# Hybrid encoder trunk: the gated branch's four tiles go straight into the projections' operand buffers

## The chip, the core and the metric

The kernel runs on one core of a Trainium2 chip. The core has five engines, each with an instruction queue that is worked off in order: PE (matrix multiplies, with its weight loads shown as PEld), DVE (elementwise and reductions), ACT (activation functions and copies with a scale), POOL (a slower elementwise engine) and SP, whose queue here only issues DMA transfers. The metric is the device time of one execution in microseconds (us); less is better.

## The reference, cut to what matters

One layer over 2048 frames of 1024 channels. Three branches (attention, a gated spatial MLP, an RWKV-7 recurrence) come out of one input projection; each is multiplied by a SiLU gate, projected to the model width, weighted by a sigmoid and summed.

```python
u, v = split(gelu(p))                       # branch B: 4 groups of 128 channels
s = einsum('gts,bnsgc->bntgc', w, layernorm(v)) + b_s
y_gm = u * s
branches = stack([y_mla, y_gm, y_rw], axis=2) * silu(z)
proj = einsum('bsnw,nwd->bsnd', branches, w_br)      # three projections, 512 -> 1024
merged = sum(proj * sigmoid(g_logit), axis=2)
x = x + gate * rmsnorm(merged @ w_out, post_g)
```

## The kernel before

**Tiling.** The 2048 frames go in four blocks `s` of 512; a tile is 128 channels by 512 frames of float32 (256 KB). Precision is kept by splitting each operand into a high and a low part: a product is three matmuls (`mm3`: high by high, high by low, low by high). `br_split` makes the parts of a projection's operand, `brh` by a copy with a scale on ACT and `brl` by a subtraction on DVE, in the pool `brp` with four buffers of each.

**Stages.** For each block there is a recurrence stage `wkv(s)` and then an attention stage `attention(s)`. Both are chains with waits in them, so a queue of independent work, `later`, is run beside them: a unit of `later` is a generator that yields wherever PE may change to another thread. The units of one queue run one after the other. In `wkv(s)` the queue holds the rest of block `s-1` (`finish_units`: `merge`, `out0`, `out1`, which end in the thread `rows`), then block `s`'s gated branch: for each group `g` the units `ug` (load the spatial result `sg_d`, compute u, multiply) and `zg` (compute the gate, multiply, store), then `operand` and eight `part` units, each a gate (24 matmuls on the 512-frame hidden state `hh`/`hl`) and a projection (12 matmuls on `brh`/`brl`).

**Order.** A planner, `Pace`, simulates the engines while the program is written out and decides which thread goes next. PE, whose order is fixed by hand, and SP's queue then run in the order that it chose. All loads and stores named here are on SP's queue; weight tiles `wh` and `wl` are prefetched there through three buffers, so an issue of a weight load waits until PE has used an older one, and everything behind it in the queue waits too.

**The lines around the change.** The unit that brings a stored branch back, used for the gated branch with `yg_d`, is

```python
def operand(src, b):
    yield ()
    for g in range(4):
        y = sm.tile([P, 512], F32, tag="z2", name="yg", bufs=3)
        SY.dma_start(y, src[g])
        b.append(br_split(y))
```

The tile `ut` that holds a gated tile has one buffer. `rows` is the end of block `s-1`: eight times it loads a tile `y` and a tile `x`, combines them on DVE, and stores `out`, with three buffers for the loads; `wkv(s)` lasts until it is done, and the attention's first loads (`stg`) are queued on SP behind its last store.

Of the kernel before, what the change touches and what calls it, by code (L numbers as in the profile page):

```python
# [11 lines left out]
F32 = mybir.dt.float32  # L12
# [9 lines left out]
P = 128  # L22
D = 1024
T = 2048
SB = 512
NSB = T // SB
# [280 lines left out]
def trunk(ctx, tc, io, out):  # L307
    nc = tc.nc
    pace = Pace()
    V, A, G, PE, SY = (pace.engine(e) for e in (nc.vector, nc.scalar, nc.gpsimd, nc.tensor, nc.sync))  # L310
    ctx.enter_context(tc.manual_schedule(engines={mybir.EngineType.PE}))

    def pool(name, bufs=1, space=None, stack=ctx):
        kw = {} if space is None else {"space": space}
        return pace.pool(stack.enter_context(tc.tile_pool(name=name, bufs=bufs, reuse_waits="tile", **kw)), bufs)
# [13 lines left out]
    dr = pool("dr", 1, DRAM)  # L329
# [250 lines left out]
    def gemm(w, c0, rhs, nk=KD, r0=0):  # L580

        yield (RD, *rhs[0])
        pace.lock = pace.cur
        o = pd()
        for kg in range(nk // 4):
            pace.early = EAR
            src = w[r0 + kg * 512:r0 + (kg + 1) * 512, c0:c0 + P].rearrange("(k p) c -> p k c", p=P)
            h, l = wgran((w.tensor.name, w.offset, r0 + kg * 512, c0), lambda raw: SY.dma_start(raw, src))
            pace.early = 0.0
            pace.forget(h, l)  # L590
            for k in range(4):
                kk = kg * 4 + k
                rh, rl = rhs[kk]
                yield (rh, rl)
                mm3(o, h[:, k, :], l[:, k, :], rh, rl, kk == 0, kk == nk - 1)
        pace.lock = None
        return o

    def silu2(n, f):

        o = yield from gemm(w_in, O_Z + n * 512 + f * P, hT)
        t = sm.tile([P, 512], F32, tag="gt", name="zt", bufs=2)
        A.activation(t, o, AF.Tanh, scale=0.5)
        z = sm.tile([P, 512], F32, tag="z2", name="z2", bufs=3)
        V.scalar_tensor_tensor(z, t, 1.0, o, op0=ALU.add, op1=ALU.mult)
        return z

    def br_split(b2, pl=brp):

        h = pl.tile([P, 512], F32R, tag="brh", name="brh", bufs=4)  # L610
        l = pl.tile([P, 512], F32R, tag="brl", name="brl", bufs=4)
        A.activation(h, b2, AF.Copy, scale=0.5)
        V.scalar_tensor_tensor(l, b2, 0.5, h.bitcast(F32), op0=ALU.mult, op1=ALU.subtract)
        return h, l
# [88 lines left out]
    yo_d = [dr.tile([8, P, SB], F32, name=f"yo_d{i}") for i in range(NSB)]  # L703
    y_d = [dr.tile([SB, D], F32, name=f"y_d{i}") for i in range(NSB)]
    yr_d = [dr.tile([4, P, SB], F32, name=f"yr_d{i}") for i in range(NSB)]
    yg_d = [dr.tile([4, P, SB], F32, name=f"yg_d{i}") for i in range(NSB)]

    def trig_of(s, pl):

# [200 lines left out]

        return [lambda f=f: vproj(f) for f in range(4)] + [vnorm] + [lambda g=g: spatial(g) for g in range(4)]

    def gm_gates(s):

        t = {}

        def ug(g):
            t[g] = sm.tile([P, 512], F32, tag="ut", name="ut", bufs=1)
            SY.dma_start(t[g], sg_d[s][g])
            o = yield from gemm(w_in, O_U + g * P, hT)  # L920
            u = sm.tile([P, 512], F32, tag="gt", name="gu", bufs=2)
            A.activation(u, o, AF.Gelu)
            V.tensor_tensor(out=t[g], in0=t[g], in1=u, op=ALU.mult)

        def zg(g):
            z = yield from silu2(1, g)
            V.tensor_tensor(out=t[g], in0=t[g], in1=z, op=ALU.mult)
            SY.dma_start(yg_d[s][g], t[g])

        return [f for g in range(4) for f in (lambda g=g: ug(g), lambda g=g: zg(g))]  # L930


    def latents():
# [15 lines left out]
    def wkv(s):  # L949
# [6 lines left out]
        with ExitStack() as st:  # L956
            pl = pool("wkv", 1, stack=st)
# [346 lines left out]

            rest = deque(later)
            later.clear()
            groups = (finish_units(s - 1, pl) if s else []) + [gm_gates(s) + branch(yg_d[s], s, 1)]
            for u in groups:
                later.append(u[0])
                for _ in range(GAP):  # L1310
# [219 lines left out]
    def gate(n, d):  # L1530
        og = yield from gemm(w_in, O_G + n * D + d * P, hT)
        t = sm.tile([P, 512], F32, tag="gt", name="gt", bufs=2)
        A.activation(t, og, AF.Tanh, scale=0.5)
        return t
# [5 lines left out]
    def part(n, s, d, br):  # L1540

        if n == 2:
            yield (lambda: s == NSB - 1 or old.get("turn", 0) > s,)
            t = sm.tile([P, 512], F32, tag="gt", name="gt", bufs=2)
            SY.dma_start(t, gd[s % 2][1][d])
            q = sm.tile([P, 512], F32, tag="z2", name="p1", bufs=3)
            SY.dma_start(q, pp[s % 2][0][d])
        else:
            t = yield from gate(n, d)
        op = yield from gemm(w_br[n], d * P, br, nk=4)  # L1550
        V.scalar_tensor_tensor(t, t, 1.0, op, op0=ALU.add, op1=ALU.mult)
        if n == 2:
            G.tensor_tensor(out=t, in0=t, in1=q, op=ALU.add)
        SY.dma_start(pp[s % 2][n - 1][d], t)
# [7 lines left out]
# [7 lines that stand above are left out]
# [5 lines left out]
    def branch(src, s, n):  # L1574

        b = []
        return [lambda: operand(src, b)] + [lambda d=d: part(n, s, d, b) for d in range(8)]
# [140 lines left out]
    with ExitStack() as st:  # L1718
        pl = pool("first", 1, stack=st)
# [5 lines left out]
    for s in range(NSB):  # L1725
        wkv(s)
        later.extend([lambda: mark(s)] + branch(yr_d[s], s, 2) + [lambda: mark(s, 2)])
        if s + 1 < NSB:
            attention(s, None)
        else:  # L1730
            with ExitStack() as st:
                bp = pool("brl", 1, stack=st)
                b0 = attention(s, bp)
                finish(s, b0)
# [23 lines left out]
```

## Time and profile before

| what | value |
|---|---|
| median of three runs | 3120.82 us (3120.63 to 3137.46) |
| the profiled execution | 3130.59 us, its span 3128.7 us |
| engines busy | PE 93%, DVE 55%, ACT 39%, POOL 19% of the span |
| DMA moved | 654.24 MB, mean 209 GB/s |
| mean granted clock of PE | 0.966 of full speed |

The span is from the first to the last instruction of the profiled execution; it is 1.9 us shorter than that execution's device time, which is itself 9.8 us (0.3%) above the median. A busy share is an average over stages; what a wait costs is read in its stage. In a timeline, a number in brackets at the end of a row is the time for which that engine sat idle before the instruction, with what ended it.

### The profile page before, as it was taken

What the parts mean: (1) busy time and instruction counts of PE and PEld (TensorE: products, weight loads), DVE (VectorE), ACT (ScalarE), POOL (GpSimd) and SP (SyncE); (2) the same over time, 40 slices, a digit from 0 to 9 for tenths busy, and PEclk for the clock granted to TensorE, in tenths of its full rate; (3) what the DMA queues carried; (4) which work ended last, traced back from release to release, by engine and by line L of the source; (5) the groups of instructions that cost most, each with busy time, mean ns of one, the idle gap of its engine ahead of it and who ended that gap; (6) DMA issues with size and microseconds to landing.
All of it is one profiled execution on the core that took longest, in us unless ns stands there. A gap on an engine that the chain in (4) does not pass through costs nothing.

```text
span 3128.7 us, 49533 instructions
## 1 busy us (share of the span) xinstructions
PE 2896.8 (93%) x16924; PEld 2337.8 (75%) x16924; DVE 1711.0 (55%) x4574; ACT 1231.6 (39%) x2866; POOL 595.7 (19%) x606
## 2 busy tenths in 40 slices
PE   5889898989989989999999998998999999899998
PEld 4667666778867767888867776887787677688886
DVE  6426666356356733467357653446645666266552
ACT  4325333444233423454233322554433333266641
POOL 3123232341121201122011101113100110122210
PEclk8999999989999989999999999999999999999999
DMA  8887765877676678766665577655557547844356
GB/s 272 264 274 240 225 191 167 281 251 242 222 221 196 196 229 280 219 205 191 212 199 174 165 243 251 207 167 188 154 170 243 182 149 227 272 151 129 125 181 208
DMA packets 525993, 654.24 MB, mean 209 GB/s; under 512 B 142673, under 2 KB 255405, under 8 KB 525741
## 3 DMA queue, kind: packets, MB, share of 16 engines
q1 hardware_dynamic: 525568, 651.03, 65.8%
q8 instruction: 134, 2.20, 0.3%
q14 instruction: 119, 0.97, 0.1%
q10 hardware_dynamic: 172, 0.05, 0.0%
HBM read 461.88 MB, written 189.01 MB: 208 GB/s over the span
## 4 chain that ended last, share of the span: by engine, by line
PE 40%; DVE 4%; DMA 3%; ACT 1%; issue 1%; SPq 1%; POOL 1%; POOLq 0%; DVEq 0%; ACTq 0%
PE pd L120 23%; PE pss L120 7%; PE pst L120 6%; PE pso L120 3%; SPq L120 1%; DVE X L120 1%; DVE tx L120 1%; DMA x<-in_x 1%; DMA yg<-yg_d 0%; DMA stg<-kp_d 0%; DMA tg<-gate_d 0%; DVE brl L120 0%; DMA stg<-q_d 0%; DMA yg<-mg_d 0%; POOL rs L120 0%
## 5 line engine op out<-in xcount | busy, mean ns | idle before, releaser
L120 PE MATMUL pd<-hh,wh 128*128 128x512 f32 x1952 | 811.3, 416 | 20.1 <-ACT wh L120 7.1
L120 PE MATMUL pd<-hh,wl 128*128 128x512 f32 x1952 | 774.9, 397 | 9.3 <-POOL wl L120 5.7
L120 PE MATMUL pd<-hl,wh 128*128 128x512 f32 x1952 | 771.7, 395 | 2.4 <-DVE hl L120 1.5
L120 PEld LDWEIGHTS pd<-hh,wh 128*128 128x128 f32 x1952 | 373.1, 191 | 112.1 <-issue 18.7
L120 PEld LDWEIGHTS pd<-hh,wl 128*128 128x128 f32 x1952 | 371.4, 190 | 98.8 <-POOL wl L120 9.8
L120 PEld LDWEIGHTS pd<-hl,wh 128*128 128x128 f32 x1952 | 373.2, 191 | 70.6 <-DVE hl L120 3.3
L120 DVE TENSOR_TENSOR pw<-pst,ph 128x512 fp32r<-128x512 f32 (+2 forms) x352 | 196.3, 568 | 246.0 <-ACT ph L120 244.7
L120 PE MATMUL pd<-brh,wh 128*128 128x512 f32 x576 | 259.5, 450 | 51.0 <-ACT brh L120 20.4
L120 ACT ACTIVATE ph<-pst 128x512 fp32r<-128x512 f32 (+2 forms) x352 | 171.5, 497 | 230.6 <-PE pst L120 199.1
L120 PE MATMUL pd<-brl,wh 128*128 128x512 f32 x576 | 236.3, 410 | 0.4 <-DVE brl L120 0.4
L120 PE MATMUL pd<-brh,wl 128*128 128x512 f32 x576 | 235.0, 408 | 0.5 <-DMA wl<-kept 0.5
L120 ACT ACTIVATE p<-p,nm 128x512 f32<-128x512 f32 (+3 forms) x288 | 189.9, 661 | 90.5 <-DVE nm L120 90.2
L120 DVE TENSOR_SCALAR_CACHE_REDUCE p<-pss 128x512 f32<-128x512 f32 (+2 forms) x320 | 191.1, 606 | 50.0 <-PE pss L120 46.3
L120 POOL TENSOR_TENSOR wl<-wr,wh 128x512 fp32r<-128x512 f32 x98 | 129.5, 1323 | 447.3 <-ACT wh L120 357.8
L120 ACT ACTIVATE wh<-wr 128x512 fp32r<-128x512 f32 x162 | 101.3, 628 | 215.7 <-PE pd L120 75.1
L120 PEld LDWEIGHTS pd<-brh,wh 128*128 128x128 f32 x576 | 113.5, 197 | 89.1 <-issue 25.0
L120 PE MATMUL pst<-consts,p 128*128 128x128 f32 x1088 | 162.5, 274 | 6.8 <-DVE t L120 3.7
L120 PE MATMUL pso<-ph,v 128*128 128x256 f32 x576 | 153.2, 288 | 0.5 <-ACT ph L120 0.5
L120 PE MATMUL pso<-pw,v 128*128 128x256 f32 x576 | 146.5, 283 | 0.1
L120 PEld LDWEIGHTS pst<-consts,p 128*128 128x128 f32 x1088 | 128.7, 141 | 23.6 <-issue 5.4
L120 POOL TENSOR_TENSOR kl<-stg,kh 96x512 fp32r<-96x512 f32 x80 | 103.3, 1293 | 210.1 <-ACT kh L120 194.5
L120 PEld LDWEIGHTS pd<-brh,wl 128*128 128x128 f32 x576 | 113.7, 197 | 27.5 <-DMA wl<-kept 0.9
(293 smaller groups left out, 4833.7 us busy)
## 6 DMA issues: line engine op xcount, KB each, us to landing
wh<-kept SPq DMA_DIRECT2D x486, 256.0 KB
wl<-kept SPq DMA_DIRECT2D x486, 256.0 KB
kept<-wh SPq DMA_DIRECT2D x162, 256.0 KB
kept<-wl SPq DMA_DIRECT2D x162, 256.0 KB
wr<-in_w_in SPq DMA_DIRECT2D x120, 256.0 KB
gate_d<-gt SPq DMA_DIRECT2D x64, 256.0 KB
part_d<-gt SPq DMA_DIRECT2D x64, 256.0 KB
p<-part_d SPq DMA_DIRECT2D x64, 256.0 KB
```

What stands on the lines that cost most here:

```text
L120: r = f(*a, **k)
```

## The change

`zg` no longer stores its tile to `yg_d`. It splits the tile into `brh` and `brl` at once and appends the pair to the list that the `part` units read. The unit `operand` is gone for this branch, and with it the reload; the other branches keep theirs. The tensor `yg_d` goes.

```diff
-    yg_d = [dr.tile([4, P, SB], F32, name=f"yg_d{i}") for i in range(NSB)]
-    def gm_gates(s):
-        t = {}
+    def gm_branch(s):
+        t, b = {}, []
         def zg(g):
             z = yield from silu2(1, g)
             V.tensor_tensor(out=t[g], in0=t[g], in1=z, op=ALU.mult)
-            SY.dma_start(yg_d[s][g], t[g])
-        return [f for g in range(4) for f in (lambda g=g: ug(g), lambda g=g: zg(g))]
+            b.append(br_split(t[g]))
+        return [f for g in range(4) for f in (lambda g=g: ug(g), lambda g=g: zg(g))] + [lambda d=d: part(1, s, d, b) for d in range(8)]
-            groups = (finish_units(s - 1, pl) if s else []) + [gm_gates(s) + branch(yg_d[s], s, 1)]
+            groups = (finish_units(s - 1, pl) if s else []) + [gm_branch(s)]
```

The planner sees other instructions, so it writes another order. SP's queue at the end of the last recurrence stage before, from the store of the fourth gated tile to the attention's first load (`yr_d` is the recurrence branch, whose reload follows):

```order
L120 DMA yg_d_370<-ut 128x512
L120 DMA yg<-yg_d_370 128x512
L120 DMA wh<-kept 128x512
L120 DMA out<-y 128x512
L120 DMA wl<-kept 128x512
L120 DMA yg<-yg_d_370 128x512 x3
...
L120 DMA out<-y 128x512
L120 DMA wl<-kept 128x512
L120 DMA wh<-kept 128x512
L120 DMA yg<-yr_d_366 128x512
L120 DMA stg<-q_d_326 96x512
```

The same place now, from the load of the fourth `ut`:

```order
L120 DMA ut<-sg_d_342 128x512
L120 DMA wl<-kept 128x512
L120 DMA out<-y 128x512
L120 DMA y<-y_d_361 128x512
L120 DMA x<-in_x 128x512
...
L120 DMA out<-y 128x512
L120 DMA wh<-kept 128x512
L120 DMA yg<-yr_d_366 128x512
L120 DMA wl<-kept 128x512
L120 DMA stg<-q_d_326 96x512
```

The stores and reloads are gone from between the `out` stores, and the attention's first load is still behind the last `out`.

DVE's queue at the same place before, around the fourth gated tile:

```order
L120 TENSOR_TENSOR ut<-ut,gu 128x512
L120 TENSOR_TENSOR ut<-ut,z_27889 128x512
L120 SCALAR_TENSOR_TENSOR y<-y,ors,x 128x512
L120 SCALAR_TENSOR_TENSOR brl<-yg,brh 128x512 x4
L120 SCALAR_TENSOR_TENSOR gt<-gt,pd 128x512
L120 SCALAR_TENSOR_TENSOR y<-y,ors,x 128x512
```

And now:

```order
L120 TENSOR_TENSOR ut<-ut,gu 128x512
L120 SCALAR_TENSOR_TENSOR y<-y,ors,x 128x512
L120 SCALAR_TENSOR_TENSOR z_27864<-zt,pd 128x512
L120 TENSOR_TENSOR ut<-ut,z_27864 128x512
L120 SCALAR_TENSOR_TENSOR brl<-ut,brh 128x512
L120 SCALAR_TENSOR_TENSOR y<-y,ors,x 128x512
L120 SCALAR_TENSOR_TENSOR gt<-gt,pd 128x512
```

The four splits that stood together behind the reload are now one behind each tile's last product, each ahead of one of the `rows` combinations (`y<-y,ors,x`).

PE's queue before, around the first score matmuls (`kh,qh`) of the last attention stage:

```order
L120 MATMUL pd<-brl,wh 128x512
L120 MATMUL pd<-brh,wl 128x512
L120 MATMUL pd<-hh,wh 128x512
L120 MATMUL pd<-hl,wh 128x512
L120 MATMUL pd<-hh,wl 128x512
L120 MATMUL pss<-kh,qh 128x512
L120 MATMUL pss<-kl,qh 128x512
```

And now:

```order
L120 MATMUL pd<-hl,wh 128x512
L120 MATMUL pd<-hh,wl 128x512
L120 MATMUL pss<-kh,qh 128x512
L120 MATMUL pss<-kl,qh 128x512
L120 MATMUL pss<-kh,ql 128x512
L120 MATMUL pd<-hh,wh 128x512
L120 MATMUL pd<-hl,wh 128x512
L120 MATMUL pd<-hh,wl 128x512
L120 MATMUL pd<-brh,wh 128x512
```

Between the stage's last `Y` transposes and its first scores stood 165 + 12 + 24 + 12 + 3 matmuls of gemms (216); now there are 165 + 12 + 21 (198). In the third block it was 219 and is 198. In the second block two `part` units and a gate stood between the gated branch and the first scores, and now it is three and a gate. In the first block the last state chunk of the first head pair is followed, before its `Y` transposes, by 24 + 12 + 24 matmuls where there were 6; in return one later pair of heads has 12 state matmuls in a row with nothing between them, where it had 8.

## Rows read from the trace of the kernel before

**Rows 1.** The page, part 1: busy time, share of the span, instructions

```profile
PE 2896.8 (93%) x16924; PEld 2337.8 (75%) x16924; DVE 1711.0 (55%) x4574; ACT 1231.6 (39%) x2866; POOL 595.7 (19%) x606
```

**Rows 2.** DMA issues by line: count, size of each

```profile
yg_d<-ut SPq DMA_DIRECT2D x16, 256.0 KB
yg<-yg_d SPq DMA_DIRECT2D x16, 256.0 KB
```

**Rows 3.** The operand's `brl` splits: ns min/median/max, first and last start

```profile
L120 DVE SCALAR_TENSOR_TENSOR brl<-yg,brh x68: 669/692/1607, 383.9 to 2871.6; 128x512 fp32r<-128x512 f32 x68
```

**Rows 4.** What PE waited for, whole span: us in total, times, longest

```profile
PE pd L120 <- ACT brh L120: 20.4, 6, 10.7
```

**Rows 5.** PE's timeline, third block, end of the recurrence stage: start us, us

```profile
1894.82 0.39 PE L120 MATMUL pd<-hh,wl 128*128 128x512 f32 x1
...
1900.94 0.39 PE L120 MATMUL pd<-hh,wl 128*128 128x512 f32 x1
1912.00 0.79 PE L120 MATMUL pd<-brh,wh 128*128 128x512 f32 x1 [10.68 <-ACT brh L120]
...
1917.36 0.40 PE L120 MATMUL pd<-hh,wh 128*128 128x512 f32 x1
...
1927.02 0.50 PE L120 MATMUL pss<-kh,qh 96*128 96x512 f32 x1 [0.62 <-ACT kh L120]
```

**Rows 6.** SP's timeline, same stage: first and last `out`, reloads, first attention load

```profile
1854.50 0.34 SPq L120 DMA_DIRECT2D out<-y  x1
...
1905.84 1.40 SPq L120 DMA_DIRECT2D yg<-yg_d  x3
...
1912.70 0.32 SPq L120 DMA_DIRECT2D yg<-yg_d  x1
...
1918.56 0.34 SPq L120 DMA_DIRECT2D out<-y  x1
...
1920.94 0.42 SPq L120 DMA_DIRECT2D stg<-q_d  x1
```

**Rows 7.** PE's timeline, fourth block, end of the recurrence stage

```profile
2704.28 0.79 PE L120 MATMUL pd<-brh,wh 128*128 128x512 f32 x1 [5.24 <-ACT brh L120]
...
2707.41 0.79 PE L120 MATMUL pd<-brh,wh 128*128 128x512 f32 x1 [1.18 <-ACT brh L120]
...
2711.59 0.39 PE L120 MATMUL pd<-hh,wh 128*128 128x512 f32 x1
...
2723.55 0.49 PE L120 MATMUL pss<-kh,qh 96*128 96x512 f32 x1 [2.93 <-ACT kh L120]
```

**Rows 8.** SP's timeline, fourth block: first and last `out`, first attention load

```profile
2651.90 0.38 SPq L120 DMA_DIRECT2D out<-y  x1
...
2713.65 0.38 SPq L120 DMA_DIRECT2D out<-y  x1
...
2715.77 0.41 SPq L120 DMA_DIRECT2D stg<-q_d  x1
```

**Rows 9.** DVE's timeline, fourth block: the first two `rows` combinations

```profile
2649.87 0.74 DVE L120 SCALAR_TENSOR_TENSOR y<-y,ors,x 128x512 f32<-128x512 f32 x1
...
2657.43 0.74 DVE L120 SCALAR_TENSOR_TENSOR y<-y,ors,x 128x512 f32<-128x512 f32 x1
```

**Rows 10.** PE's timeline, second block: the first projection of the gated branch

```profile
1202.36 0.49 PE L120 MATMUL pd<-brh,wh 128*128 128x512 f32 x1 [0.41 <-ACT brh L120]
...
1207.06 0.79 PE L120 MATMUL pd<-brh,wh 128*128 128x512 f32 x1 [2.53 <-ACT brh L120]
...
1211.15 0.63 PE L120 MATMUL pd<-hh,wh 128*128 128x512 f32 x1
```

**Rows 11.** DVE's timeline, first block: a split of the gated branch

```profile
388.66 1.38 DVE L120 SCALAR_TENSOR_TENSOR brl<-yg,brh 128x512 fp32r<-128x512 f32 x1 [0.29 <-ACT brh L120]
```

**Rows 12.** PE's timeline, first block: the wait for `Y` of the first head pair

```profile
393.95 1.09 PE L120 MATMUL pss<-consts,Y 128*128 128x128 f32 x4 [8.17 <-DVE Y L120]
```

**Rows 13.** Ten us after the stop in the third block: PE, PEld, DVE, ACT, POOL, PEclk, DMA

```profile
1910.00:1920.00 10.00, 7.84 (x24) 5.62 (x25) 4.07 (x6) 2.53 (x4) 0.00 (x0) 0.69 0.75 269
```

## The prediction

> **What bounds the kernel now.** The page's first part comes first: PE is busy 93% of the span and DVE, next, 55% [rows 1]. Independent work is put beside both chains, so the change can pay only in those stretches where PE stood still or ran at a lower clock, and the question for each edit is whether PE waited for it. The second view is the list of PE's waits: the largest single group is PE waiting for `brh`, 20.4 us in 6 waits, the longest 10.7 [rows 4]. The third is PE's timeline, which tells whose `brh` that was. It is the gated branch's, and three blocks share it: 10.68 us in the third [rows 5], 5.24 and 1.18 in the fourth [rows 7], 0.41 and 2.53 in the second [rows 10]; that is 20.0 of the 20.4. In the first block no such wait shows; there PE stands 8.17 us for `Y` of the recurrence [rows 12]. The last view is SP's queue in the same stretches, since a reload is issued there among weight loads and the transfers of `rows`.
>
> The sum is made against the profiled execution, 3130.6 us; it lies 0.3% above the median of 3120.8, and I take the difference found on the one off the other. A change of under 1% (31 us) can hardly be told from none here.
>
> **What goes.** 16 stores and 16 reloads of 256 KB [rows 2], 8.4 MB of 654 MB. The 20 us above are their round trip: the fourth tile cannot be reloaded before its store has landed, and PE has only the first gate's 24 matmuls to do meanwhile. Bytes by themselves I price at nothing, since none of the waits above is for bandwidth as such; the range takes in what shorter queues would give.
>
> **What stays.** The 16 splits on ACT and DVE are the same operations on the same shapes, 0.69 us on DVE [rows 3]. They move from behind the reload to behind each tile's last product. In DVE's queue each now stands ahead of one of the `rows` combinations, so a late `brh` on ACT holds up `rows`. The price is between nothing and a split with a wait like the one of 0.29 us [rows 11], about 1.0 us each, at most eight times in the last two blocks: 0 to 8 us. I take 0, because the four splits stood in the same queue before, in a clump, and waited there too. SP's wait for the last product and for the landing of the store goes with the store; `ut` is now released by the split, not by the store's landing. Four buffers of each half are filled one after the other while the gates are computed; the queue of independent work is one thread, so no other branch asks for them meanwhile, and nothing is priced for that.
>
> **Second block.** The first projection's 12 matmuls begin at 1202.36 after 0.41 us of waiting and the next gate begins at 1211.15 [rows 10]: 8.79 us. At full speed a matmul follows the last in 0.227 us (27 steps from 1894.82 to 1900.94 [rows 5]), 12 in 2.72. So 6.5 us go, stops and lower clock together. Before the first scores there is now one more `part` unit, so PE has work while the attention's loads come. Gain 6.5, bounds 0 and 6.5.
>
> **Third block.** Here I don't count the 10.68 us. The attention's first load is queued behind the last `out` [rows 6], and PE's order puts its first scores 21 matmuls earlier than before (219 became 198 behind `Y`), so PE will reach them early and wait there. What decides is how fast `rows` runs. Its eight `out` stores took from 1854.50 to 1918.56, 64.1 us; held up, for one thing, because SP stood until 1912.70 at the fourth reload, with the last `y` and `x` behind it [rows 6]. One undisturbed round of `rows` took 7.56 us (2649.87 to 2657.43 [rows 9]), and a round in which three pairs of weight tiles are loaded can't be shorter than the 36 matmuls that use them up, 8.16 us. In the new order of SP's queue the seven rounds hold 2, 2, 3, 3, 2, 2 and 2 pairs: 5 x 7.56 + 2 x 8.16 = 54.1. The scores can start 10.0 us earlier, and PE has 21 x 0.227 = 4.8 us of work less behind it by then. Gain 5.2. Bounds: -4.8 if `rows` takes as long as before, and 13.2 if nothing stands in PE's way (10.68 and the 2.5 us lost from 1912.00 to 1917.36, 5.36 us for 12 matmuls).
>
> **Fourth block.** The same: `out` from 2651.90 to 2713.65, 61.75 us [rows 8]; the new rounds hold 3, 2, 3, 3, 2, 2 and 2 pairs, 54.7. The scores move 7.05 us ahead with 18 matmuls (4.1 us) undone: gain 3.0. Bounds -4.1 and 9.8 (5.24 and 1.18, and 12 matmuls in 6.13 us of the rest [rows 7] for 2.72). PE will then wait some 10 us in front of the scores where it waited 2.93 [rows 7].
>
> **First block.** The new order puts 60 matmuls (13.6 us) ahead of `Y` where PE stood 8.17 us [rows 12]. But that work is lacking later: a following pair of heads has 12 state matmuls with nothing between, for 8. The real shortening is that DVE no longer has a split of 1.38 us inside this chain [rows 11]. Gain 1.4, bounds -8.2 (the wait comes back elsewhere, and longer) and 8.2.
>
> **Sum.** 1.4 + 6.5 + 5.2 + 3.0 = 16.1 us, 0.5%: 3120.8 - 16.1 = 3105 (3114.5 in a profiled execution like this one).
>
> **The clock.** After the stop in the third block the granted clock of the next ten us was 0.69 of full speed [rows 13], between the two levels of 1.2 and 2.4 GHz, and the 12 matmuls behind it took about twice their time. My terms for the last two blocks let the new stop in front of the scores lose as much as the old one did. The Trainium skill, "TensorE: Matmul & The Clock Gate", Part 1 with its section on HAM oscillation, speaks against the change in just this way: throttled is the default state and activity lifts it, so a wait that is moved and not removed pays for the clock once more. By it the sum stays at 16; were the new stops free of it, 2.5 and 3.4 us would come on top, 3099.
>
> **The rivals.**
> - *Given back whole.* The first scores wait for `rows`, and its rounds get no shorter than what PE has left undone: the third and fourth block give nothing, the second 6.5 and the first 1.4. 3113. For it: SP's queue has the same weight loads in it, each waiting for PE; against it: SP's visible stand at the reloads.
> - *Slower.* In the third and fourth block PE, whose order is fixed, stops at scores that it meets 21 and 18 matmuls early, while `rows` keeps its 64 and 62 us and the splits ahead of its combinations make it up to 8 us longer. -4.8 - 4.1 - 8 with 6.5 + 1.4 of the others: 9 us slower, 3130. It decides against the change from the point where the rounds gain under 0.7 us each in the third block and 0.6 in the fourth. For it: the order itself; against it: SP no longer stands at the reloads between the last rounds.
> - *Nothing takes the wait's place.* Every stop named goes, with its clock: 8.2 + 6.5 + 13.2 + 9.8 = 37.7, 3083. It needs `rows` to be done 20 us earlier, for which there is no room: eight rounds are a chain of load, combination, store and load.
> - *The change doesn't do what it says.* It does in the order: 16 splits from `ut`, no transfer of `yg_d`. No chance is kept for it.
>
> **How the numbers follow.** The forecast (gain of 10 to 24 us) 0.5; given back whole 0.2; slower 0.13; nothing in its place 0.1; a new order that costs or gives more than any of these, in the first two blocks where it differs most, 0.07, two thirds of it slower. The range leaves out most of the third rival's far end and of the last case: 3088 to 3130. Faster by over 1% means under 3089.6: part of the case with nothing in its place, 0.09. Slower by over 1% means over 3152, which no row here prices: 0.04. Within 1%: 0.87.
>
> **What would show it.** In the profile of the changed kernel PE's waits for `brh` should fall from 20.4 us to under 5. In the third and fourth block the eight `out` stores should take about 54 us, and PE should wait 8 to 11 us for `kh` or `qh` in front of the first scores, with a lower clock behind. In the second block the 12 matmuls of the first projection should take 2.7 us. If the `out` stores take 62 to 64 us as before, the slower rival is right; if PE finds no wait at the scores, my reading that `rows` holds them is wrong, and the gain is larger. The wait of 8.17 us for `Y` should be gone, and smaller ones should stand later in the first block; if their sum is 8 us larger or smaller, that term is wrong.

## The result, and the profile after

The changed kernel takes 3098.75 us (median of 6 runs, 3084.82 to 3106.88) beside 3121.43 us for the kernel before on the same chip; the ratio is 0.9904, 95% interval 0.9879 to 0.993. The forecast was 3105 in 3088 to 3130: the sign and the range held. The gain was put at 16 us; it is 23 by the medians, 30 by the ratio, which is of the means (22 to 38), and 28 where the same two kernels were timed again (3096.5 beside 3124.85). The profiled execution after takes 3098.93 us, 31.7 less than the one shown of before, which was itself 9.2 us above its median. Stretches that two kernels share word for word differ by up to 6 us between their profiles, so terms below are read to that grain.

The page's first part, after, as [rows 1]:

```profile
PE 2877.7 (93%) x16924; PEld 2330.6 (75%) x16924; DVE 1714.8 (55%) x4574; ACT 1235.2 (40%) x2868; POOL 598.8 (19%) x606
```

PE does the same 16,924 matmuls in 19.1 us less, and the span is 32.1 shorter, so in these two profiles only 13.0 us of the gain are time in which PE stood still; the rest is shorter busy time, at a mean granted clock of 0.970 beside 0.966 of full speed. That split is rough: a kernel that has the order of before in its first two blocks (third and fourth block alone, below) was busy 11.1 us longer there than the profile of before. The list of what PE waited for (total, times, longest):

```profile
PE pss L120 <- DMA xtb<-xd: 34.4, 13, 11.1
PE pss L120 <- ACT kh L120: 15.2, 3, 7.5
...
PE pss L120 <- DVE Y L120: 6.1, 6, 1.6
```

The 20.4 us for `brh` [rows 4] are gone from the list altogether. Other waits grew: `kh` from 3.5 to 15.2 and `xtb`, a load of the recurrence, from 19.4 to 34.4. The two `kh` waits that matter, on PE's timeline at the first scores of the third and the fourth block, as [rows 5, 7]:

```profile
1901.20 0.80 PE L120 MATMUL pss<-kh,qh 96*128 96x512 f32 x1 [7.02 <-ACT kh L120]
...
2690.25 0.79 PE L120 MATMUL pss<-kh,qh 96*128 96x512 f32 x1 [7.45 <-ACT kh L120]
```

SP's timeline there, first and last `out` store and first attention load, third block and then fourth, as [rows 6, 8]:

```profile
1840.54 0.34 SPq L120 DMA_DIRECT2D out<-y  x1
...
1891.67 0.34 SPq L120 DMA_DIRECT2D out<-y  x1
1893.51 0.42 SPq L120 DMA_DIRECT2D stg<-q_d  x1
...
2628.15 0.38 SPq L120 DMA_DIRECT2D out<-y  x1
2680.33 0.34 SPq L120 DMA_DIRECT2D out<-y  x1
2682.21 0.38 SPq L120 DMA_DIRECT2D stg<-q_d  x1
```

The eight stores take 51.1 and 52.2 us (before 64.1 and 61.75). The most useful table cuts the span at the same instruction near the start of each recurrence stage and at each first score: in turn recurrence and attention of the second, third and fourth block (stretch; length; busy time and count of PE, PEld, DVE, ACT, POOL; PEclk; DMA share; GB/s). Before:

```profile
847.90:1225.64 377.74, 346.68 (x2218) 268.16 (x2217) 215.14 (x591) 120.08 (x297) 62.84 (x59) 0.94 0.70 219
1225.64:1565.34 339.70, 335.27 (x1786) 282.77 (x1784) 179.31 (x504) 150.92 (x351) 65.63 (x70) 0.99 0.67 213
1565.34:1927.02 361.68, 332.93 (x2196) 256.92 (x2195) 205.18 (x584) 106.69 (x272) 37.61 (x39) 0.96 0.65 206
1927.02:2368.13 441.11, 421.12 (x2254) 355.40 (x2254) 222.20 (x600) 201.49 (x469) 85.05 (x89) 0.98 0.59 186
2368.13:2723.55 355.42, 330.42 (x2197) 255.34 (x2196) 205.05 (x584) 106.58 (x272) 37.74 (x39) 0.97 0.66 210
2723.55:3117.49 393.94, 384.93 (x2201) 332.98 (x2201) 215.11 (x609) 218.06 (x527) 83.41 (x80) 0.99 0.51 159
```

After:

```profile
846.55:1209.28 362.73, 340.41 (x2253) 264.82 (x2253) 214.85 (x591) 121.18 (x298) 64.38 (x60) 0.98 0.73 228
1209.28:1554.43 345.15, 335.80 (x1773) 282.58 (x1771) 178.92 (x504) 153.72 (x353) 65.18 (x69) 0.98 0.66 208
1554.43:1901.20 346.77, 322.50 (x2176) 249.97 (x2175) 204.68 (x583) 106.18 (x271) 36.97 (x39) 0.98 0.66 206
1901.20:2343.32 442.12, 424.52 (x2275) 358.99 (x2275) 223.94 (x601) 201.34 (x470) 85.02 (x89) 0.98 0.60 188
2343.32:2690.25 346.93, 323.47 (x2179) 251.21 (x2178) 204.28 (x583) 106.27 (x271) 37.71 (x39) 0.98 0.66 207
2690.25:3085.36 395.11, 387.12 (x2219) 334.92 (x2219) 215.17 (x610) 217.67 (x528) 83.57 (x80) 0.99 0.52 161
```

Second block -15.0 and +5.5, so 9.6 us won; third -14.9 and +1.0, 13.9; fourth -8.5 and +1.2, 7.3; the first block, by the start of the second (847.90 and 846.55), 1.4. These are the forecast's four terms, 6.5, 5.2, 3.0 and 1.4. The first block's 1.4 comes with 23 matmuls fewer done by then (3306, before 3329), 5.2 us of work, which the second block does in addition. In the third and fourth recurrence stage PE's idle time (length less busy) falls by only 4.5 and 1.5 us, since the new stop at the scores stands in it; its busy time falls by 10.4 and 7.0, of which the 21 and 18 undone matmuls explain 4.8 and 4.1.

Two kernels described below, with the change in the first or in the second block alone, run PE and SP in the order of before from 1522 us on; the changed kernel timed again, and the one with the third and fourth block changed, run in that of after. The third recurrence stage in these four, in this order:

```profile
1552.92:1911.03 358.11, 330.25 (x2197) 255.16 (x2196) 205.15 (x584) 106.70 (x272) 37.17 (x39) 0.97 0.66 208
1560.15:1916.07 355.92, 328.58 (x2197) 253.73 (x2196) 205.39 (x584) 106.69 (x272) 37.21 (x39) 0.98 0.67 209
1555.14:1900.72 345.58, 323.89 (x2175) 250.91 (x2175) 204.63 (x583) 106.35 (x271) 37.03 (x39) 0.98 0.65 206
1570.57:1915.94 345.37, 322.11 (x2175) 249.81 (x2174) 204.71 (x583) 106.10 (x271) 37.08 (x39) 0.98 0.66 207
```

So part of the 14.9 belongs to the one profile of before. In the mean of three profiles of either order the third block, recurrence and attention, takes 798.2 and 787.1 us, and the fourth, to the end, 761.4 and 752.4: gains of 11.1 and 8.9.

### The profile page after: what moved, and what is told of

It is laid out like the page before. It is cut to its first block, busy times and chain, and to the rows that moved or that the text cites. A ratio compares the mean times of both kernels' runs of the same rounds, so it can differ in the third digit from the quotient of the medians.

```text
span 3096.6 us, 49478 instructions
## 1 busy us (share of the span) xinstructions
PE 2877.7 (93%) x16924; PEld 2330.6 (75%) x16924; DVE 1714.8 (55%) x4574; ACT 1235.2 (40%) x2868; POOL 598.8 (19%) x606
## 4 chain that ended last, share of the span: by engine, by line
PE 59%; DVE 5%; DMA 4%; ACT 2%; issue 1%; POOL 1%; SPq 1%; POOLq 0%; DVEq 0%; ACTq 0%
PE pd L120 36%; PE pss L120 10%; PE pst L120 9%; PE pso L120 4%; DMA x<-in_x 1%; SPq L120 1%; DVE X L120 1%; DVE tx L120 0%; DMA tg<-gate_d 0%; DMA wr<-in_w_out 0%; DMA wl<-kept 0%; DMA yo<-yo_d 0%; ACT Y L120 0%; DMA xtb<-xd 0%; DMA wh<-kept 0%
## 5 line engine op out<-in xcount | busy, mean ns | idle before, releaser
L120 PE MATMUL pd<-hh,wh 128*128 128x512 f32 x1952 | 810.6, 415 | 16.7 <-ACT wh L120 6.4
L120 PEld LDWEIGHTS pd<-hh,wh 128*128 128x128 f32 x1952 | 373.3, 191 | 105.5 <-issue 13.2
L120 PE MATMUL pd<-brh,wh 128*128 128x512 f32 x576 | 252.3, 438 | 18.8 <-DVE gt L120 9.0
L120 PE MATMUL pss<-kh,qh 96*128 96x512 f32 (+2 forms) x320 | 129.3, 404 | 18.2 <-ACT kh L120 15.2
```

The costliest lines, as they stand in the source:

```text
L120: r = f(*a, **k)
```

## The experiments

**The theory** after this reading: a reload costs by where it stands in SP's queue, ahead of `rows`' last stores and the attention's first loads, which PE waits for. The gain of the third and fourth block is these loads' earlier start. **Rivals**: PE's wait for the reloaded data alone made the cost; or the new order, which differs everywhere, made the gain.

**One part at a time.** Three kernels make the change in some blocks only:

```diff
-            groups = (...) + [gm_gates(s) + branch(yg_d[s], s, 1)]
+            groups = (...) + [gm_branch(s) if s in (2, 3) else gm_gates(s) + branch(yg_d[s], s, 1)]
```

with `(2, 3)`, `(1,)` and `(0,)`: third and fourth block, second, first.

> The change in the third and fourth block alone; blocks one and two keep the store and the reload, and PE's order up to there is that of the kernel before. Theory (each block's gain comes from its own stop at the reload and from the rounds of rows behind it): the eight out stores take 51 to 53 us in both blocks as in the changed kernel, the first scores come 7 and 5.5 us earlier against equal work, and the whole is 13 to 21 us faster than before, 3100 to 3108. Rival (the gain is the luck of a new order in the first two blocks): under 6 us faster, 3115 or more.

> The change in the second block alone. Theory: no stop for brh in the gated branch's first projection there, and 6.5 to 15 us faster than before by the first scores of that block, 3106 to 3115 at the end. Rival (the luck of the order in the first block carries it): within 4 us of the kernel before.

> The change in the first block alone, where PE did not wait for brh. Theory: the wait of 8 us for Y goes and comes back as smaller ones in the same stage, 0 plus or minus 4 us, 3117 to 3125. Rival (order): 10 us or more faster.

Measured: third and fourth block 0.9932 of before (0.9911 to 0.9953), 3108.23 us; second 0.998 (0.9966 to 0.9995), 3123.28; first 0.9961 (0.9943 to 0.9979), 3116.79; before on that chip 3129.43.

With the last two blocks alone, PE's order up to the third block's end is that of before, and the gain comes where the change is: the end of the queue on SP and the list of PE's waits there read

```profile
1906.46 0.34 SPq L120 DMA_DIRECT2D out<-y  x1
1908.30 0.42 SPq L120 DMA_DIRECT2D stg<-q_d  x1
```

```profile
PE pss L120 <- ACT kh L120: 12.9, 2, 6.8
```

with the eight stores in 49.8 and 52.2 us. From the last `Y` of the third recurrence to the start of the fourth it wins 13.1 us against the profile shown of before, from the last `Y` of the fourth to the end 7.8 (11.1 and 8.2 against the three profiles with the order of before). By the medians it wins 21 us, the theory's upper end, and the rival, luck of a new order in the first two blocks, is refuted. Inside the last two blocks the change brings a new order as well; the runs further below hold it fixed.

With the second block alone the stop for `brh` there goes and its stores take 56.1 us instead of 69.4; 9.7 us in the profile, 6 in the medians. The interval, 2 to 11 us, does not part the theory's 6.5 from the rival's 4. With the first block alone my expectation missed, and the kernel is 12.6 us faster by the medians, as the rival said: the first block itself gives nothing (its end comes 3.2 us earlier with 24 matmuls fewer done, which are 5.4 us), but the second block, whose code is that of before, becomes 9.3 us shorter. Its independent work was dealt out anew. The three parts sum to 1.27%, the whole gives 0.96%; the two don't differ beyond their intervals. By the profiles the first and the second block's parts win the same time in the second block (9.3 and 9.7 us; the whole change 9.6).

**Order alone.** The kernel before, with one number of the planner changed:

```diff
-MARG = 0.2
+MARG = 0.25
```

> The kernel before with one number of the planner changed (its margin 0.25 instead of 0.2): the same work, transfers and buffers in another order. It measures what a new order alone is worth. If the gain of the second block was order (independent work saved in one block and used in another), such a change too moves the time, by 5 to 20 us in either direction, with stretches between landmarks that differ by 5 to 15 us and cancel in part. If an order of the same planner is worth little, the time stays within 5 us and the stretches within 5. The store and reload stay, so PE's wait for brh in the third and fourth block should stay near 17 us in either case.

1.003 of before (1.0014 to 1.0047): 3133.78 us beside 3124.85, 9 us slower, and PE waits 17.8 us for `brh`. Its second block is 8.5 us longer, its third 8.4 shorter (1 to 2 against the two other profiles with the order of before there). So 8 to 9 us in the second block can be order, in either direction; what they gained here can't be split between order and the wait by these runs.

**The transfers put back.** First where the planner sees them: after `br_split(t[g])` a store to `yg_d`, and a unit of four reloads that nobody reads.

> The changed kernel with the 16 stores and 16 reloads of the gated tiles put back as transfers that nothing reads: the operands are still split where they are made. Theory (the transfers' places in SP's queue slow rows, and rows holds the first scores): the eight out stores take 58 to 64 us again in the third and fourth block, PE waits more than before in front of the scores, and only the second block's stop stays saved: 3108 to 3122. Rival (the whole cost was PE waiting for the reloaded operand; the traffic costs nothing): as fast as the changed kernel, 3095 to 3102.

0.9946 of before (0.9924 to 0.9967), about 0.4% behind the changed kernel. The stores take 64.5 and 63.5 us again, as the theory said, but the planner put 51 matmuls more than before between the third block's last `Y` and its first scores (269, before 218), so that most of their length was covered. A mixed verdict, which is why the next two hold PE's order fixed: the planner isn't told.

```diff
             b.append(br_split(t[g]))
+            nc.sync.dma_start(yg_d[s][g], t[g])
+        def reload():
+            yield ()
+            for g in range(4):
+                y = yx.tile([P, 512], F32, tag="yx", name="yx", bufs=2)
+                nc.sync.dma_start(y, yg_d[s][g])
-        return [...zg(g))] + [lambda d=d: part(1, s, d, b) for d in range(8)]
+        return [...zg(g))] + [reload] + [lambda d=d: part(1, s, d, b) for d in range(8)]
```

> The changed kernel once more, beside the next three on one chip, so that a few tenths of a per cent can be read against it. Both theories: 0.988 to 0.993 of the kernel before, the eight out stores of the third and fourth block in 50 to 54 us, PE's longest wait for kh 6 to 9 us.

> The changed kernel with the 16 stores of the gated tiles to memory and 16 reloads put back on SP's queue as dead traffic: nobody reads the reloaded tiles, and they are issued behind the planner's back, so that PE's order stays word for word that of the changed kernel. Theory (transfers that wait in SP's queue hold up rows, and rows sets the first scores): the out stores of the third and fourth block take 58 to 66 us instead of 51 to 52, PE waits 10 to 18 us for kh or qh before these scores instead of 7.5 at most, and the kernel is 8 to 20 us slower than the changed one. Rival (the reloads cost only because PE needed their data; the queue doesn't matter): out stores within 2 us of the changed kernel's and the time within 4 us of it. If the stores lengthen and the time doesn't follow, rows is not what sets the first scores.

The changed kernel on that chip: 3096.5 us, 0.991 of before (0.9889 to 0.9931). With the transfers: 3118.57 us, 0.9979 (0.9967 to 0.9992). 22 of the 28 us gained on that chip are gone again, although PE never needs the data, so the rival that its wait for the data alone made the cost is refuted. But not as I expected: in the last two blocks the stores take 50.8 and 52.9 us, so `rows` isn't lengthened there. SP's timeline at the end of the third recurrence shows what is:

```profile
1905.54 0.34 SPq L120 DMA_DIRECT2D out<-y  x1
1905.93 0.42 SPq L930 DMA_DIRECT2D yg_d<-ut  x1
1906.41 1.24 SPq L936 DMA_DIRECT2D yx<-yg_d  x2
...
1911.06 1.18 SPq L936 DMA_DIRECT2D yx<-yg_d  x2
1912.29 0.42 SPq L120 DMA_DIRECT2D stg<-q_d  x1
```

The reloads came to stand behind the last `out` and ahead of the attention's first load, which follows 6.8 us after the store instead of 1.9; the first scores come 4.9 us later there and 4.5 in the fourth block. The second loses 6.8 between its last `Y` and its scores, and there `rows` is lengthened: the reloads stand among its stores, which take 68.9 us instead of 53.1, and PE, which found no wait at these scores in the changed kernel, waits 6.64 us for `kh`. The first loses 7.9 between two `Y`, with the granted clock at 0.83 instead of 0.93; whether that last loss is the reloads', one profile can't tell. So the last two blocks lose about half of what the change won in them and the first two all of it; that the sums are near each other is no proof that the same terms went.

The same kernel with `[reload]` moved behind the eight `part` units:

> The kernel with the dead stores and reloads (16 of each on SP's queue, PE's order that of the changed kernel), with only the place of the reloads moved: behind the eight part units instead of ahead of them, so in the last two blocks behind the attention's first loads. Theory (a reload costs by standing, with its wait for the store, ahead of the attention's first loads in SP's queue; its bytes cost nothing): the first attention load of the third and fourth block follows the last out store within 2 to 3 us again, the delay of the first scores there falls from 4.9 and 4.5 us to under 1.5 each, and the kernel is 8 to 14 us faster than with the reloads ahead. Rival (bytes, or any 16 more waits in the queue, wherever they stand): within 4 us of that kernel, 0.996 to 1.000 of the kernel before.

3097.07 us beside 3125.0, 0.9904 of before (0.9888 to 0.9919): as fast as the changed kernel, with the same stores, reloads and bytes as the kernel that is 0.7% slower. So the place in the queue costs, and the bytes alone don't. Where the place costs came out otherwise than expected. In the third block the first load does follow the last store at once, but PE still waits at the scores of the third and the fourth block (7.36 and 7.68 us before the move):

```profile
1839.20 0.34 SPq L120 DMA_DIRECT2D out<-y  x1
...
1894.29 0.34 SPq L120 DMA_DIRECT2D out<-y  x1
1896.14 0.46 SPq L120 DMA_DIRECT2D stg<-q_d  x1
```

```profile
1902.22 0.79 PE L120 MATMUL pss<-kh,qh 96*128 96x512 f32 x1 [5.52 <-ACT kh L120]
...
2693.87 0.80 PE L120 MATMUL pss<-kh,qh 96*128 96x512 f32 x1 [7.75 <-ACT kh L120]
```

The eight stores now take 55.1 and 55.4 us, and the first scores stand 55.1 and 56.1 us behind the last `Y`, where they stood 55.2 and 56.3 with the reloads ahead and 50.3 and 51.9 in the changed kernel. So the expected fall of that delay to under 1.5 us is missed: in the last two blocks this profile wins nothing by the move. The 16.7 us by which it is shorter lie in the first block (7.3) and in the second (11.5, and 2.1 are given back elsewhere), where the stores take 62.3 us instead of 68.9 and PE finds no wait at the scores. Shown is, then, that the reloads' place costs, and in the second block by way of `rows`. That a place between the last store and the attention's first loads costs by itself is not shown; why the stores of the last two blocks grew is open, and this one profile is 6.4 us above its kernel's median.

What all profiles with these loads on SP agree on is that the first scores of the third and the fourth block stand 5.6 to 9.6 us behind the first load, wherever it stands (42 to 59 us behind the last `Y`).

**Four buffers** for `rows`: `FB = 3` becomes `FB = 4`.

> The changed kernel with four buffers instead of three for rows' loads (and whatever else has that size). Theory (a round of rows is a chain of load, combination and store through three buffers): the out stores of the third and fourth block come closer, 40 to 48 us, PE's 15.2 us of waiting for kh fall under 8, and the kernel is 5 to 12 us faster than the changed one. Rival (SP's queue sets the rounds, since each weight pair between two rounds waits for PE): out stores 49 to 54 us as now, time within 4 us of the changed kernel. The planner writes another order for it, so a difference under 6 us in either direction proves neither.

0.9895 (0.9877 to 0.9914) beside 0.991 on the same chip; the stores take 47.7 and 52.8 us. The time fits the rival, and so does the fourth block; the third is within the theory's 40 to 48. So the buffers aren't shown to set the rounds, nor shown not to: the order is a new one, and a difference this small was said beforehand to prove neither. Counting weight-tile loads between two `out` stores does better: in the changed kernel's third block rounds with four of them take 5.7 to 7.4 us and with five or six 7.3 to 8.6, 33 in all; before, 35, and the last round with four of them took 13.1, because the reloads stood in it.

**More matmuls.** Is work left over for the attention stage free, as the attention's lengths above suggest (441.1 and 442.1 us with 21 more)? In the third and the fourth attention, 14 times:

```diff
+                    for _ in range(3):
+                        nc.tensor.matmul(o, h[:, k, :], rh, start=True, stop=True)
                 mm3(o, h[:, k, :], l[:, k, :], rh, rl, kk == 0, kk == nk - 1)
```

> The changed kernel with 42 matmuls too many in each of the third and the fourth attention stage: the first matmul of 14 gemms is issued three times more (it starts the sum anew, so the result is the same), unseen by the planner. 84 matmuls of 0.227 us are 19 us. Theory now (work that is left over for an attention stage falls into PE's idle slots there and costs nothing, as the 21 and 18 matmuls left over by the change seemed to): under 6 us slower than the changed kernel. Rival (my forecast's: what is left over must be paid): 15 to 20 us slower, 0.996 to 0.998 of the kernel before. In between: the slots take up part of it, and the share is the answer.

0.9969 (0.9957 to 0.9981), 3115.26 us, 17 to 18 slower than the two neighbours on its chip. The theory falls: 42 matmuls more cost 8.6 us in the third stage and 12.0 in the fourth, where 9.5 is their full price. Why the third block's left-over ones were nearly free is seen in the first 20 and the next 20 us behind its first scores, before and after:

```profile
1927.02:1947.02 20.00, 17.38 (x71) 13.27 (x72) 8.60 (x30) 13.13 (x32) 10.24 (x12) 0.91 0.64 189
1947.02:1967.02 20.00, 18.66 (x101) 15.28 (x101) 8.31 (x27) 11.27 (x29) 4.24 (x4) 1.00 0.87 276
```

```profile
1901.20:1921.20 20.00, 18.78 (x73) 14.86 (x74) 7.80 (x26) 12.20 (x32) 9.42 (x11) 0.80 0.69 204
1921.20:1941.20 20.00, 20.00 (x108) 17.24 (x107) 9.73 (x29) 11.03 (x29) 3.83 (x4) 1.00 0.85 272
```

Before, PE stood 4.0 of these 40 us; after, 1.2. It gets through 9 more matmuls there even at the lower clock. So 2.8 us of the 4.8 went into idle time at the start of the stage; for the other 2 no row speaks, and they are within the grain of two profiles. The fourth block has no such slot (PE stood 1.1 us in its first 40 before, 0.9 after). Over three profiles of either order the third attention grew by 1.6 us of the 4.8 left over, and the fourth by 3.1 of the 4.1: there the work was paid for the most part.

**The first loads on another queue.** What PE still waits for at the first scores:

```diff
-                        SY.dma_start(x[r0:r0 + src.shape[0]], src)
+                        (G if h == 0 else SY).dma_start(x[r0:r0 + src.shape[0]], src)
```

> The changed kernel with the q and k loads of an attention stage's first head issued on POOL's queue instead of SP's; the planner counts them as before, so that PE's order stays that of the changed kernel. Theory (what PE still waits for at the first scores, 12.9 to 15.2 us of kh in three stages, is the place of these loads behind the last out store on SP): the loads start before the last out store, the waits for kh in the third and fourth block fall from 5 to 7 us each to under 2, the first scores come 4 to 6 us earlier in each, and the kernel is 8 to 14 us faster than the changed one, 0.986 to 0.989 of the kernel before. Rival (the tiles of the attention stage lie in memory that rows or the recurrence still uses, so the loads wait for the last combinations on any queue): within 3 us of the changed kernel. Third case: POOL, which also makes the low parts, is held up by waiting for the loads' buffers, and the kernel is slower than the changed one.

0.9911 (0.9897 to 0.9924): no change, and PE waits 6.2 and 6.4 us at the scores. POOL issued the third block's loads 46 us ahead of the last `out` store, behind which they stand on SP, and ACT shows what then came last:

```profile
1840.99 0.61 POOL L120 DMA_DIRECT2D stg<-q_d  x1
```

```profile
1884.23 0.62 ACT L120 ACTIVATE qh<-stg 96x512 fp32r<-96x512 f32 x1
1894.44 0.89 ACT L120 ACTIVATE v<-vf 128x256 fp32r<-128x256 f32 x2 [9.59 <-DMA vf<-v_d]
1895.24 0.61 ACT L120 ACTIVATE kh<-stg 96x512 fp32r<-96x512 f32 x1
```

The copy that makes `kh` stands on ACT behind that of `v`, whose load was still on SP. So that load was moved too:

> As the kernel before it, but the first head's v loads (vf) go over POOL's queue too. There the q and k loads were issued 40 us early and PE still waited 6 us: on ACT the copy of v, whose load was still on SP behind the last out store, stood ahead of the copy that makes kh. Theory (the first scores are held by whichever load of the first head is still on SP): the waits for kh at the third and fourth block's first scores fall from 6 us to under 2, PE's wait at the fourth is gone or moved to the second key tile, the scores come 4 to 6 us earlier in each, and the kernel is 8 to 12 us faster than the changed one, 0.986 to 0.989 of the kernel before. Rival (PE, once past this wait, stops at the next load a little later for as long): the first scores earlier, the end of the attention stage not, within 4 us of the changed kernel.

0.994 (0.9918 to 0.9961), some 9 us slower than the changed kernel. In the third block ACT's next instruction is now a sum over `x`, loaded on SP, and it waits 10 us with `kh` behind it. In the fourth the first scores do come without a wait and 7.6 us earlier behind the last `Y`, more than the theory's 4 to 6, and PE stops at a later pair of tiles:

```profile
2694.56 0.39 PE L120 MATMUL pss<-kh,qh 96*128 96x512 f32 x1
...
2711.91 0.48 PE L120 MATMUL pss<-kh,qh 96*128 96x128 f32 x1 [7.31 <-ACT kh L120]
```

In the 20 us from the first of these rows it stands 11.8. The rival, a stop a little later, holds in kind, though the kernel is slower than the 4 us that it allowed. No version beats the changed kernel by more than the runs can tell.

## Why the prediction was right, and which terms were off

- **What bounds the kernel.** Right in the main: `brh` was the group to read, its waits went, and part of the time went into new stops at the first scores. The wait of 10.68 became 7.02 and that of 5.24 became 7.45, in front of the scores, for `kh`; I had said 8 to 11. What the 10.68 were I misread: not the landing of the fourth tile's store. SP, ACT and DVE in the kernel before:

```profile
1866.62 0.42 SPq L120 DMA_DIRECT2D yg_d<-ut  x1
...
1911.32 1.97 ACT L120 ACTIVATE brh<-yg 128x512 fp32r<-128x512 f32 x3 [9.36 <-DMA yg<-yg_d]
...
1911.98 2.03 DVE L120 SCALAR_TENSOR_TENSOR brl<-yg,brh 128x512 fp32r<-128x512 f32 x3 [6.56 <-ACT brh L120]
```

  PE waited for the first tile. Its store was issued at 1866.62, but the unit `operand` comes behind all four tiles, so its reload was issued at 1905.84 and ACT had it 5.5 us later. The fourth reload, at 1912.70 [rows 6], was held until the first split was done (1911.98 and some 0.7 us), since the reloads share three buffers.
- **The transfers themselves at nothing.** Right for the whole, by the runs with the reloads behind the `part` units. Block by block it isn't shown: beside the changed kernel's two profiles that one's last two blocks are 4 to 7 us longer from the last `Y` on, its second 5.7 shorter.
- **Third and fourth block, 8.2 us.** The mechanism was right (the wait isn't won, the earlier start of the attention's first loads is), the size too small: 21 us with these blocks changed alone by ratio (15 to 28), 20 by three profiles of either order. Two sizes were off. The stores took 51.1 and 52.2 us, not 54.1 and 54.7: I had given a round with two weight pairs the 7.56 us of one undisturbed round [rows 9], which is the step between two combinations; between its stores the same round took 6.56 (2651.90 to 2658.46), and the last ones took 5.7 to 7.0 (before, the reloads stood in them). And I charged all 21 and 18 left-over matmuls, 8.9 us. In the third block only 1.6 of 4.8 were paid; in the fourth, 3.1 of 4.1, the charge was nearly right. The upper bounds, 13.2 and 9.8, lay nearer to the 11.1 and 8.9 (the 2.5 us in the first of them are 2.64 by its own rows, 5.36 less 2.72).
- **Why the rounds were slow before.** Half right. A reload between two stores does hold a round up, 13.1 us for one that takes 6.4 without. But with the dead reloads behind the last store, the stores kept their pace and the first loads were late all the same; with those moved away, the stores were slower and the loads as late. The first scores followed the first load in every one of these kernels, and `rows` is only one of the things ahead of it. How the 20 us of these two blocks divide between the place of the reloads and PE's need of the data stays open: the dead reloads cost some 9 us there (4.9 and 4.5).
- **Second block, 6.5.** The 12 matmuls of the first projection take 2.72 us, as said, from the first row to the next gate:

```profile
1184.80 0.39 PE L120 MATMUL pd<-brh,wh 128*128 128x512 f32 x1
...
1187.52 0.39 PE L120 MATMUL pd<-hh,wh 128*128 128x512 f32 x1
```

  The block won 9.6, and that with 22 matmuls more done, 5.0 us of work; my bound was 6.5. The rest is the stores in 53.2 us instead of 69.4 and a new deal of independent work, which I had not priced outside the last case. The part that changes the first block alone shows such a deal to be worth as much by itself.
- **First block, 1.4.** The number, 1.4 by its end, agrees by luck: it is within the grain of two profiles, and 23 matmuls fewer were done by then, 5.2 us, so at equal work the block won nothing. The wait of 8.17 for `Y` went, and waits for `xtb` (12.7 us in 5 between 330 and 600) took its place.
- **The splits ahead of `rows` at nothing.** Right: there are 16, of 0.69 us as before, and those of the third block waited 0.70 us for `brh` at most:

```profile
L120 DVE SCALAR_TENSOR_TENSOR brl<-ut,brh x16: 682/692/980, 279.0 to 2675.3; 128x512 fp32r<-128x512 f32 x16
```

- **The clock.** The new stop does cost clock behind it: 0.80 of full speed in the 20 us behind the third block's first scores, 0.91 before. The mean of the recurrence stage ahead of it rose from 0.96 to 0.98, though (in the two other kernels with the order of before it is 0.97 and 0.98), and over three profiles of either order PE's busy time in the third and fourth stage fell by 3.0 and 4.6 us more than the undone matmuls explain. So the new stop seems to lose less than the old ones, where I had put both equal; the difference is no larger than the grain. The Trainium skill, "TensorE: Matmul & The Clock Gate", Part 1 with HAM oscillation, leads one to expect a moved wait to pay again: the trace agrees in kind; whether in amount too, these profiles can't tell.
- **The rivals.** *Given back whole* and *slower* both needed `rows` to keep its length, or to shorten by no more than the left-over work; its stores shortened by 12.9 and 9.6 us. *Nothing in its place* is refuted by the 7.02 and 7.45 us. And a change of under 1% could be told from none after all: the ratio's interval is 0.5% wide.

## What to carry to other kernels

A round trip through memory can cost by the place of its waiting transfers in an in-order queue, even where nobody needs their data: look at what stands behind them, a chain's other transfers or a next stage's first loads. Before pricing a round of a chain from one undisturbed instance, count what else the queue has to issue in it; before charging work that is left for a later stage, look whether that stage stands idle at its start, which is not the whole stage. Where a planner writes the order, an edit in one block can pay in another: change one block at a time, and measure a new order with nothing else changed. And where a run comes out as a theory said, look whether its profile has the gain in the place that the theory named.

## What was not expected of the hardware

Issuing the q and k loads on POOL's queue put them 46 us ahead (1840.99, the last `out` store of that execution being at 1887.35), and nothing came of it. The Trainium skill, "DMA: Bandwidth & Descriptors", section "Issuing engines are not separate DMA queues", says that starting transfers on several engines only saves the time to initiate them; here it also let them pass a queue that was waiting, so the trace shows more than the page, yet the end didn't move, because ACT, in order too, stood 9.59 us for the next load on SP. And 8.4 MB of dead transfers, 16 stores and 16 reloads, cost nothing that 0.3% could show where the reloads stood behind the `part` units, and 0.7% where they stood ahead.
